# Copying the strided operands of dilated attention scores into contiguous tiles

## The chip, the cores and the metric

One NeuronCore of one Trainium2 chip runs the whole program in one launch. The metric is the device time in microseconds (us); the kernel was run several times and the median counts. One more execution was taken with the profiler on, and all rows shown here are from that one.

## The reference

A decoder trunk of two layers on a sequence of 2048 tokens with 1024 features, in float32. The second layer has, beside four retention heads, eight heads of dilated attention of 64 features each. The part that matters here:

```
DIL_PATTERNS = ((128, 1), (512, 4), (2048, 16))      # (window, dilation)

for window, dil in DIL_PATTERNS:
    # query t attends keys t, t-dil, ..., t-window (causal)
    # tokens are gathered by residue class mod dil, then cut into blocks of 128 queries
    s = q_block @ [previous block | own block of keys].T / 8
    p = exp(s - max), den = sum(p), o = p @ v / den, lse = max + log(den)
o = sum over patterns of softmax(lse) * o
```

With dilation 1 there are 16 blocks of consecutive tokens. With dilation 4 a block is every fourth token of a stretch of 512, so there are four stretches with four residues each. With dilation 16 a block is every sixteenth token of the whole sequence, and there is no previous block.

## The kernel before, in words

**Number format.** Products that need float32 accuracy are made from f16 numbers split into a high and a low part. A head's operands are in one SBUF tile, `st`, of shape [128 partitions, 3, 2048 tokens]. `st[:, 0]` holds the queries, their high part in partitions 0 to 63 and their low part in 64 to 127; `st[:, 1]` the keys' high part in both halves, `st[:, 2]` the keys' low part in both. Two matmuls per score block (lines 892 and 893), one with `st[:, 1]` and one with `st[:, 2]`, add up to the score. For dilation 4 and 16 both take their queries and keys out of `st` with a step of 4 or 16 tokens.

**Groups.** `groups(h)` makes 12 groups of four score blocks for head h: 0 to 3 for dilation 1 (pattern 0), 4 to 7 for dilation 4 (pattern 1, one stretch of 512 tokens each, four residues), 8 to 11 for dilation 16 (pattern 2, four residues each). A score block is 128 queries by 256 keys (128 where there is no previous block). The order within a head is 4 to 11, then 0 to 3.

**One group.** `scores` runs eight matmuls on TensorE into a PSUM tile `big` (two buffers); VectorE adds the mask and takes the row maximum (L895), and makes the bias (L898); ScalarE takes the exponential and the row sum (L899) and converts to f16, `dl_ph` (L901); VectorE subtracts to get the low part, `dl_pl` (L902); two DMA transposes issued by SyncE bring both into `dl_pt` (L903, L904). `values`, two groups later (`LAG`), multiplies `dl_pt` with the values on TensorE (L914, L915), and ScalarE (L918) and VectorE (L921) write the sum of the two halves of the result into the head's record `dl_rec`. Records of patterns 1 and 2 go through device memory to be put in token order (L928, L929, issued by GpSimd). `mixed` joins the three patterns (L935 to L955; the products of L952 run on GpSimd). `dl_ph`, `dl_pl`, `dl_pt` and the score tile `dl_s` have two buffers each; `dl_o1` has one.

**What runs between the groups.** `periods` and `merge` put other units of work between the groups of a head, by a written cost: the projection of the next head (`Heads.tiles`: products of `co.rows`, L164 to L166, then rope on VectorE, L762 to L765, an addition on GpSimd, L766, evacuation on ScalarE, L406 and L407, and DMA transposes into the next head's `st`, L421) and projections of the gate and of the retention inputs (`Extra.rows`: the same products, evacuation by ScalarE, L230 or L233, and a store issued by GpSimd, L234). These projections go through the PSUM tile `dn` (two buffers).

**Order.** The program is written in this order, and the framework (`TileContext(..., schedule_with_timeline_sim=True)`) sets every semaphore and decides at build time, with its own estimates of durations, in which order each engine gets its instructions. At run time each engine works through its own list in order, and an instruction that waits holds up those behind it. A tile name with k buffers can be given out again when the last reader of the tile k allocations before is done.

Of the kernel before, what the change touches and what calls it, by code (L numbers as in the profile page):

```python
# [7 lines left out]
F32 = mybir.dt.float32  # L8
F16 = mybir.dt.float16
BF16 = mybir.dt.bfloat16  # L10
I32 = mybir.dt.int32
AF = mybir.ActivationFunctionType
# [5 lines left out]
S = 2048  # L18
# [831 lines left out]
def dilated(co, work, keep, heads, cst, v_d, rec_d, mix_d):  # L850

    nc = co.nc
    mask = work.tile([128, 256], F32, name="dl_mask", bufs=1)
    nc.sync.dma_start(mask, cst["c_dmask"])
    recs, live = {}, {}

    def groups(h):
        v1 = heads.v[h]
        nc.gpsimd.dma_start(v_d[h].rearrange("(t p) n -> p t n", p=128), v1)
        v2 = work.tile([128, 4, 4, 128], F16, name="dl_v2", bufs=1)  # L860
        nc.gpsimd.dma_start(v2, v_d[h].rearrange("(b i r) n -> i b r n", b=4, r=4))
        v3 = work.tile([128, 16, 128], F16, name="dl_v3", bufs=1)
        nc.gpsimd.dma_start(v3, v_d[h].rearrange("(i r) n -> i r n", r=16))
        out = []
        for t0 in range(0, NT, 4):
            ts = [1, 2, 3, 0] if t0 == 0 else range(t0, t0 + 4)
            out.append((0, [(t, slice(128 * t, 128 * t + 128), slice(128 * max(t - 1, 0), 128 * t + 128),
                             [v1[:, k, :] for k in ((t - 1, t) if t else (0,))]) for t in ts]))
        for b in range(4):
            out.append((1, [(4 * b + r, slice(512 * b + r, 512 * b + 512, 4),  # L870
                             slice(512 * max(b - 1, 0) + r, 512 * b + 512, 4),
                             [v2[:, k, r, :] for k in ((b - 1, b) if b else (0,))]) for r in range(4)]))
        for r0 in range(0, 16, 4):
            out.append((2, [(r, slice(r, S, 16), slice(r, S, 16), [v3[:, r, :]]) for r in range(r0, r0 + 4)]))
        recs[h] = [keep.tile([128, NT, 66], F32, name=f"dl_rec{i}", bufs=2 if i == 1 else 1) for i in range(3)]
        return out

    def scores(h, g, pat, units):
        rec, st, f = recs[h][pat], heads.st[h], heads.f[h]
        p = co.ps([128, 1024], "big")  # L880
        raw = work.tile([128, 1024], F32, name="dl_s")
        ph = work.tile([128, 1024], F16, name="dl_ph")
        pl = work.tile([128, 1024], F16, name="dl_pl")
        pt = work.tile([128, 2, 8, 128], F16, name="dl_pt")
        m = co.small.tile([128, 4], F32, name="dl_m")
        at, spans = 0, []
        for n, qs, ks, vs in units:
            width = 128 * len(vs)
            sp = slice(at, at + width)
            spans.append(sp)  # L890
            at += width
            nc.tensor.matmul(p[:, sp], st[:, 0, qs], st[:, 1, ks], start=True, stop=False)  # L892
            nc.tensor.matmul(p[:, sp], st[:, 0, qs], st[:, 2, ks], start=False, stop=True)  # L893
        for i, ((n, _, _, vs), sp) in enumerate(zip(units, spans)):
            nc.vector.tensor_tensor_reduce(  # L895
                out=raw[:, sp], in0=p[:, sp], in1=mask[:, 256 - 128 * len(vs):], scale=f[:, 0:1],
# [10 lines left out]
    def values(h, g, pat, units):  # L907
# [3 lines left out]
        for i, ((n, _, _, vs), sp) in enumerate(zip(units, spans)):  # L911
            for k, x in enumerate(vs):
# [1 line left out]
                nc.tensor.matmul(pv[:, i, :], pt[:, 0, kt, :], x, start=k == 0, stop=False)  # L914
                nc.tensor.matmul(pv[:, i, 0:64], pt[:, 1, kt, :], x[:, 0:64], start=False,  # L915
                                 stop=k == len(vs) - 1)
        o1 = work.tile([128, 4, 64], F32, name="dl_o1", bufs=1)
        nc.scalar.activation(o1, pv[:, :, 0:64], AF.Copy)  # L918
        ns = [un[0] for un in units]
        if ns == sorted(ns):  # L920
            nc.vector.tensor_add(rec[:, ns[0]:ns[0] + 4, 0:64], pv[:, :, 64:128], o1)  # L921
        else:
            nc.vector.tensor_add(rec[:, 1:4, 0:64], pv[:, 0:3, 64:128], o1[:, 0:3, :])
            nc.vector.tensor_add(rec[:, 0:1, 0:64], pv[:, 3:4, 64:128], o1[:, 3:4, :])
        if pat and g % 4 == 3:
            rd = rec_d[h, pat - 1]
            lay = ("(b i r) n -> i b r n", "(i b r) n -> i b r n")[pat - 1]
# [292 lines left out]
```

## Time and profile before

| what | us |
|---|---|
| median of 3 runs | 2388.01 (2387.26 to 2394.36) |
| the profiled execution, its own time | 2393.75 |
| span of the profiled execution, first to last instruction | 2391.7 |
| TensorE (PE) busy in the span | 2186.1 |
| VectorE (DVE) busy | 1549.6 |
| ScalarE (ACT) busy | 1121.3 |
| GpSimd (POOL) busy | 531.3 |
| dilated scores, first to last matmul | 1272.0 to 2062.0 |

PE is TensorE's matmuls, PEld its weight loads, DVE is VectorE, ACT ScalarE, POOL GpSimd, SP SyncE; a q behind an engine's name means its sequencer, which issues DMAs and waits. L892 is line 892 of the kernel before. Matmuls overlap: the duration of one is longer than the distance to the next.

### The profile page before, as it was taken

What the parts mean: (1) busy time and instruction counts of PE and PEld (TensorE: products, weight loads), DVE (VectorE), ACT (ScalarE), POOL (GpSimd) and SP (SyncE); (2) the same over time, 40 slices, a digit from 0 to 9 for tenths busy, and PEclk for the clock granted to TensorE, in tenths of its full rate; (3) what the DMA queues carried; (4) which work ended last, traced back from release to release, by engine and by line L of the source; (5) the groups of instructions that cost most, each with busy time, mean ns of one, the idle gap of its engine ahead of it and who ended that gap; (6) DMA issues with size and microseconds to landing.
All of it is one profiled execution on the core that took longest, in us unless ns stands there. A gap on an engine that the chain in (4) does not pass through costs nothing. (4 is left out here: it accounts for less than half of the span.)

```text
span 2391.7 us, 51539 instructions
## 1 busy us (share of the span) xinstructions
PE 2186.1 (91%) x19956; PEld 1694.2 (71%) x19956; DVE 1549.6 (65%) x4870; ACT 1121.3 (47%) x2580; POOL 531.3 (22%) x638
## 2 busy tenths in 40 slices
PE   4888799998999999999999998999998799889998
PEld 3666687676687878754448978888887688765454
DVE  5447666666676768566557675667574667687674
ACT  5445445454555546345444544555453445533332
POOL 0012211212212012111112122231322122145441
PEclk9799899999999999999999999999998899989999
DMA  9958888988898867888877687786786858966653
GB/s 203 177 109 152 150 152 151 176 151 144 157 162 167 152 141 181 217 194 211 216 168 143 138 143 149 136 165 145 143 145 120 139 114 159 168 214 181 178 171 106
DMA packets 840501, 381.87 MB, mean 160 GB/s; under 512 B 743088, under 2 KB 799296, under 8 KB 840000
## 3 DMA queue, kind: packets, MB, share of 16 engines
q1 hardware_dynamic: 742832, 259.29, 57.6%
q0 software_dynamic: 23584, 82.33, 12.6%
q10 hardware_dynamic: 73840, 36.97, 6.5%
q8 instruction: 156, 2.56, 0.4%
q14 instruction: 89, 0.73, 0.1%
HBM read 135.40 MB, written 73.73 MB: 87 GB/s over the span
## 5 line engine op out<-in xcount | busy, mean ns | idle before, releaser
L164 PE MATMUL dn<-w,uh 128*128 128x192 f16 (+1 forms) x3840 | 1010.4, 263 | 19.1 <-DVE x_out L231 6.6
L166 PE MATMUL dn<-w,ul 128*128 128x192 f16 (+1 forms) x3840 | 1009.0, 263 | 4.7 <-DMA ul<-u_lo 4.7
L165 PE MATMUL dn<-w,uh 128*128 128x192 f16 (+1 forms) x3840 | 1009.5, 263 | 0.0
L164 PEld LDWEIGHTS <-uh 128*128 128x128 f16 x3968 | 394.3, 100 | 54.4 <-DMA uh<-u_hi 16.2
L166 PEld LDWEIGHTS <-ul 128*128 128x128 f16 x3968 | 392.1, 100 | 42.4 <-DMA ul<-u_lo 15.3
L165 PEld LDWEIGHTS <-uh 128*128 128x128 f16 x3968 | 393.3, 100 | 35.6 <-issue 7.5
L516 ACT ACTIVATE fx_s<-fx_s,fx_nm 128x1152 f32<-128x1152 f32 (+15 forms) x128 | 152.7, 1194 | 182.0 <-DVE fx_nm L514 182.0
L899 ACT ACTIVATE dl_s<-dl_s,dl_m 128x256 f32<-128x256 f32 (+1 forms) x384 | 172.6, 451 | 118.7 <-DVE dl_m L898 103.4
L521 DVE TENSOR_TENSOR fx_pl<-fx_s,fx_ph 128x2176 f16<-128x2176 f32 x64 | 155.0, 2423 | 82.0 <-DMA fx_tl<-fx_pl 47.9
L895 DVE CUSTOM_DVE_ANT_0 dl_s<-big,dl_mask,hd_f 128x256 f32<-128x256 f32 (+1 forms) x384 | 141.7, 420 | 52.9 <-PE big L893 51.8
L508 DVE CUSTOM_DVE_ANT_0 fx_s<-big,cb,hd_f 128x1024 f32<-128x1024 f32 (+7 forms) x128 | 133.6, 1044 | 34.5 <-PE big L506 20.2
L79 POOL TENSOR_TENSOR rs_r<-rs_v,mhalf 128x1 f32<-128x1 f32 (+2 forms) x96 | 67.4, 706 | 396.4 <-DVE rs_v L76 377.3
L902 DVE TENSOR_TENSOR dl_pl<-dl_s,dl_ph 128x512 f16<-128x512 f32 (+2 forms) x96 | 100.5, 1049 | 78.7 <-ACT dl_ph L901 58.5
L520 ACT ACTIVATE fx_ph<-fx_s 128x2176 f16<-128x2176 f32 x64 | 128.8, 2012 | 32.9 <-DMA fx_th<-fx_ph 25.5
L503 PE MATMUL big<-head 128*128 128x512 f16 (+3 forms) x320 | 113.2, 354 | 28.0 <-DVE fx_m L508 27.9
L85 DVE SCALAR_TENSOR_TENSOR w<-w_raw,w_gs,w 128x256 f16<-128x256 f32 (+2 forms) x296 | 123.9, 472 | 12.4 <-ACT w L84 12.3
L892 PE MATMUL big<-head 128*128 128x256 f16 (+1 forms) x384 | 129.5, 355 | 0.6 <-DVE dl_rec L895 0.6
L893 PE MATMUL big<-head 128*128 128x256 f16 (+1 forms) x384 | 129.7, 357 | 0.0
L84 ACT ACTIVATE w<-w_raw,w_gs 128x256 f16<-128x256 f32 (+2 forms) x296 | 113.5, 466 | 30.5 <-DVE w_gs L145 23.1
L536 PE MATMUL aux<-head,fx_tl 128*128 128x64 f16 x1088 | 105.7, 197 | 22.8 <-DMA fx_tl<-fx_pl 22.7
L535 PE MATMUL aux<-head,fx_th 128*128 128x128 f16 x1088 | 110.4, 224 | 16.9 <-DMA fx_th<-fx_ph 16.9
L547 POOL TENSOR_TENSOR fx_o<-fx_o 128x64 f32<-128x64 f32 x128 | 46.3, 381 | 333.8 <-DVE fx_o L541 193.1
(235 smaller groups left out, 4332.1 us busy)
## 6 DMA issues: line engine op xcount, KB each, us to landing
gate_d<-x_out POOLq DMA_DIRECT2D x64, 256.0 KB, 4.0
o_gate<-gate_d SPq DMA_DIRECT2D x32, 512.0 KB, 4.4
rec_d<-dl_rec POOLq DMA_DIRECT2D x16, 528.0 KB, 5.4
dl_rec<-rec_d POOLq DMA_DIRECT2D x16, 528.0 KB, 6.1
x_h<-in_x_dram SPq DMA_DIRECT2D x16, 512.0 KB, 4.6
cb<-cum_d SPq DMA_DIRECT2D x16, 512.0 KB, 10.3
o_mix<-mix_d SPq DMA_DIRECT2D x32, 256.0 KB, 3.0
o_h<-in_x_dram SPq DMA_DIRECT2D x16, 512.0 KB, 4.6
```

Source lines behind the costliest of these rows:

```text
L85: self.nc.vector.scalar_tensor_tensor(lo, x, scale, hi, op0=OP.mult, op1=OP.subtract)
L164: nc.tensor.matmul(out, uh[:, k, xs], wh[:, k, c0:c1], start=k == 0, stop=False)
L165: nc.tensor.matmul(out, uh[:, k, xs], wl[:, k, c0:c1], start=False, stop=False)
L166: self.last = nc.tensor.matmul(out, ul[:, k, xs], wh[:, k, c0:c1], start=False, stop=k == KT - 1)
L508: nc.vector.tensor_tensor_reduce(out=x[:, at + c * 1024:at + c * 1024 + wide], in0=p[:, :wide], in1=cb[c][:, :wide], scale=f[:, 0:1], scal ...
L516: nc.scalar.activation(x[:, sp], x[:, sp], AF.Exp, bias=nm[:, part:part + 1], accum_out=nm[:, 2 + part:3 + part])
L520: nc.scalar.activation(ph, x[:, 0:W], AF.Copy)
L521: nc.vector.tensor_sub(pl, x[:, 0:W], ph)
L892: nc.tensor.matmul(p[:, sp], st[:, 0, qs], st[:, 1, ks], start=True, stop=False)
L893: nc.tensor.matmul(p[:, sp], st[:, 0, qs], st[:, 2, ks], start=False, stop=True)
L895: nc.vector.tensor_tensor_reduce(out=raw[:, sp], in0=p[:, sp], in1=mask[:, 256 - 128 * len(vs):], scale=f[:, 0:1], scalar=-3.0e38, op0=OP. ...
L899: nc.scalar.activation(raw[:, sp], raw[:, sp], AF.Exp, bias=m[:, i:i + 1], accum_out=rec[:, n, 65:66])
```

## The change

For patterns 1 and 2 a new function, `stage`, copies a group's queries (`dl_gq`, one buffer) and both key parts (`dl_gk`, two buffers) out of `st` into tiles in which the 128 tokens of a score block are contiguous. GpSimd makes the copies. The score matmuls read these tiles. Since the previous key block of a dilation-4 group lies in the tile of the group before, a block of 256 keys is computed as two of 128, with two matmuls each. `dl_ph` and `dl_pl` go from two buffers to one. The tile `dl_o1` goes: ScalarE writes the first half of the values' result straight into the record and VectorE adds the second half in place; where the group's blocks are out of order (the first group of pattern 0) both do it in two pieces.

```diff
-    recs, live = {}, {}
+    recs, live, staged = {}, {}, {}
...
         for b in range(4):
-            out.append((1, [(4 * b + r, slice(512 * b + r, 512 * b + 512, 4),
-                             slice(512 * max(b - 1, 0) + r, 512 * b + 512, 4),
+            out.append((1, [(4 * b + r, None, None,
                              [v2[:, k, r, :] for k in ((b - 1, b) if b else (0,))]) for r in range(4)]))
         for r0 in range(0, 16, 4):
-            out.append((2, [(r, slice(r, S, 16), slice(r, S, 16), [v3[:, r, :]]) for r in range(r0, r0 + 4)]))
+            out.append((2, [(r, None, None, [v3[:, r, :]]) for r in range(r0, r0 + 4)]))
...
+    def stage(h, g):
+
+        st = heads.st[h]
+        src = (st[:, :, 512 * (g - 4):512 * (g - 3)].rearrange("p s (i r) -> p s r i", r=4) if g < 8
+               else st.rearrange("p s (i r) -> p s r i", r=16)[:, :, 4 * (g - 8):4 * (g - 7), :])
+        ks = work.tile([128, 2, 4, 128], F16, name="dl_gk")
+        nc.gpsimd.tensor_copy(ks, src[:, 1:3])
+        qs = work.tile([128, 4, 128], F16, name="dl_gq", bufs=1)
+        nc.gpsimd.tensor_copy(qs, src[:, 0])
+        staged[h, g] = qs, ks
+
     def scores(h, g, pat, units):
         rec, st, f = recs[h][pat], heads.st[h], heads.f[h]
+        if pat:
+            stage(h, g)
         p = co.ps([128, 1024], "big")
         raw = work.tile([128, 1024], F32, name="dl_s")
-        ph = work.tile([128, 1024], F16, name="dl_ph")
-        pl = work.tile([128, 1024], F16, name="dl_pl")
+        ph = work.tile([128, 1024], F16, name="dl_ph", bufs=1)
+        pl = work.tile([128, 1024], F16, name="dl_pl", bufs=1)
...
-            nc.tensor.matmul(p[:, sp], st[:, 0, qs], st[:, 1, ks], start=True, stop=False)
-            nc.tensor.matmul(p[:, sp], st[:, 0, qs], st[:, 2, ks], start=False, stop=True)
+            if pat == 0:
+                nc.tensor.matmul(p[:, sp], st[:, 0, qs], st[:, 1, ks], start=True, stop=False)
+                nc.tensor.matmul(p[:, sp], st[:, 0, qs], st[:, 2, ks], start=False, stop=True)
+                continue
+            q = staged[h, g][0][:, n % 4, :]
+            for i in range(len(vs)):
+                ks = staged[h, g - len(vs) + 1 + i][1]
+                kp = slice(sp.start + 128 * i, sp.start + 128 * (i + 1))
+                nc.tensor.matmul(p[:, kp], q, ks[:, 0, n % 4, :], start=True, stop=False)
+                nc.tensor.matmul(p[:, kp], q, ks[:, 1, n % 4, :], start=False, stop=True)
...
-        o1 = work.tile([128, 4, 64], F32, name="dl_o1", bufs=1)
-        nc.scalar.activation(o1, pv[:, :, 0:64], AF.Copy)
         ns = [un[0] for un in units]
-        if ns == sorted(ns):
-            nc.vector.tensor_add(rec[:, ns[0]:ns[0] + 4, 0:64], pv[:, :, 64:128], o1)
-        else:
-            nc.vector.tensor_add(rec[:, 1:4, 0:64], pv[:, 0:3, 64:128], o1[:, 0:3, :])
-            nc.vector.tensor_add(rec[:, 0:1, 0:64], pv[:, 3:4, 64:128], o1[:, 3:4, :])
+        for a, b in ((0, 4),) if ns == sorted(ns) else ((0, 3), (3, 4)):
+            to = rec[:, ns[a]:ns[b - 1] + 1, 0:64]
+            nc.scalar.activation(to, pv[:, a:b, 0:64], AF.Copy)
+            nc.vector.tensor_add(to, pv[:, a:b, 64:128], to)
```

## Rows read from the trace of the kernel before

**Rows 1.** The page, busy engines, and TensorE's granted clock in 40 slices.
```profile
PE 2186.1 (91%) x19956; PEld 1694.2 (71%) x19956; DVE 1549.6 (65%) x4870; ACT 1121.3 (47%) x2580; POOL 531.3 (22%) x638
...
PEclk9799899999999999999999999999998899989999
```

**Rows 2.** Windows: stretch, length, busy us per engine, clock, DMA share.
```profile
1272.00:2070.00 798.00, 747.83 (x7619) 660.64 (x7617) 530.95 (x2216) 409.44 (x1266) 188.50 (x202) 0.97 0.75 142
2070.00:2392.00 322.00, 293.94 (x1688) 169.10 (x1685) 217.58 (x630) 101.90 (x196) 129.11 (x108) 0.96 0.60 169
```

**Rows 3.** Waits of TensorE, 1272 to 2070: total us, times, longest.
```profile
PE aux L914 <- DMA dl_pt<-dl_ph: 23.4, 3, 11.2
PE aux L915 <- DMA dl_pt<-dl_pl: 22.8, 13, 5.9
```

**Rows 4.** Timeline of TensorE: start, duration; a pattern-1 group with 256 keys.
```profile
1607.04 0.39 PE L892 MATMUL big<-head 128*128 128x256 f16 x1
...
1608.86 0.29 PE L164 MATMUL dn<-w,uh 128*128 128x256 f16 x1
```

**Rows 5.** Timeline of TensorE: a pattern-1 group with 128 keys.
```profile
1586.28 0.28 PE L892 MATMUL big<-head 128*128 128x128 f16 x1
...
1587.20 0.24 PE L914 MATMUL aux<-head,dl_pt 128*128 128x128 f16 x1
```

**Rows 6.** Timeline of TensorE: a pattern-2 group.
```profile
1625.47 0.40 PE L892 MATMUL big<-head 128*128 128x128 f16 x1
...
1627.37 0.27 PE L164 MATMUL dn<-w,uh 128*128 128x192 f16 x1
```

**Rows 7.** Timeline of TensorE: a value pair, then a pattern-0 group.
```profile
1352.89 0.22 PE L914 MATMUL aux<-dl_v,dl_pt 128*128 128x128 f16 x1
...
1352.97 0.22 PE L914 MATMUL aux<-dl_v,dl_pt 128*128 128x128 f16 x1
...
1353.22 0.27 PE L892 MATMUL big<-head 128*128 128x256 f16 x1
...
1353.88 0.22 PE L892 MATMUL big<-head 128*128 128x128 f16 x1
...
1353.99 0.27 PE L164 MATMUL dn<-w,uh 128*128 128x256 f16 x1
```

**Rows 8.** Groups by line and shape, GpSimd: busy us, mean ns, idle before.
```profile
L482 POOL TENSOR_SCALAR cb<-cb,hd_f 128x1024 f32<-128x1024 f32 x16 | 46.7, 2919 | 90.7 <-DMA cb<-cum_d 84.3 <-PE dn L166 6.4
L952 POOL TENSOR_TENSOR dl_rec<-dl_rec,dl_es 128x1024 f32<-128x1024 f32 x24 | 46.5, 1956 | 42.0 <-DVE dl_es L949 18.6 <-ACT dl_o L918 9.4 <-DVE dl_m L898 7.8
...
L234 POOL DMA_DIRECT2D qkv_d<-x_out x32 | 23.3, 728 | 114.2 <-ACT x_out L233 85.9 <-ACT dl_o L918 28.4
...
L929 POOL DMA_DIRECT2D dl_rec<-rec_d x16 | 18.9, 1179 | 67.4 <-DMA rec_d<-dl_rec 42.3 <-issue 8.2 <-DVE dl_rec L924 5.8
```

**Rows 9.** Waits of GpSimd, 1272 to 2070: total us, times, longest.
```profile
POOL qkv_d L234 <- ACT x_out L233: 85.9, 20, 7.3
...
POOL dl_rec L929 <- DMA rec_d<-dl_rec: 42.3, 10, 12.7
```

**Rows 10.** Waits of ScalarE, 1272 to 2070.
```profile
ACT dl_ph L901 <- DMA dl_pt<-dl_ph: 38.5, 7, 15.7
```

**Rows 11.** The tile dl_ph: durations as min, median, max ns; landing of its transposes.
```profile
L901 ACT ACTIVATE dl_ph<-dl_s x96: 612/996/1061, 1286.0 to 2072.7; 128x1024 f16<-128x1024 f32 x48, 128x512 f16<-128x512 f32 x40, 128x896 f16<-128x896 f32 x8
...
DMA to landing us min/median/max: 2.4/3.5/18.5
```

**Rows 12.** Waits of SyncE's DMA queue, 1272 to 2070.
```profile
SPq L903 <- PE aux L915: 145.7, 40, 12.6
```

**Rows 13.** Timelines of VectorE and GpSimd near 1592 us; line 902 in all.
```profile
1592.48 1.24 DVE L902 TENSOR_TENSOR dl_pl<-dl_s,dl_ph 128x512 f16<-128x512 f32 x1 [1.27 <-ACT dl_ph L901]
...
1591.28 4.21 POOL L952 TENSOR_TENSOR dl_rec<-dl_rec,dl_es 128x1024 f32<-128x1024 f32 x2 [2.17 <-DVE dl_es L949]
...
L902 DVE TENSOR_TENSOR dl_pl<-dl_s,dl_ph x96: 675/1210/2780, 1291.3 to 2073.8; 128x1024 f16<-128x1024 f32 x48, 128x512 f16<-128x512 f32 x40, 128x896 f16<-128x896 f32 x8
```

## The prediction

> **What bounds the kernel now.** I read the page first: TensorE is busy 91% of the span and its granted clock is close to full in nearly all of the 40 slices [rows 1]. Then I cut the span into stretches. All the scores that the change touches run between 1272 and 2070 us, one third of the span, which I call the stage. In it TensorE is busy 748 of 798 us at a clock of 0.97, VectorE 531, ScalarE 409 and GpSimd 188 [rows 2]. So TensorE sets the pace of the stage and the others have room; the 322 us behind it hold none of the changed work. The waits of TensorE tell where its missing 50 us are: 23.4 and 22.8 us before the value products, on the transposes that bring the probabilities into dl_pt [rows 3]. The reader should keep that in mind, because the change touches the buffers in front of these transposes.
>
> **What the scores cost.** Matmuls overlap, so I take the distance from start to start. Eight matmuls of pattern 1 with 256 strided columns (every 4th element) take from 1607.04 to 1608.86, 1.82 us [rows 4]. In its first block, with 128 columns, eight take 0.92 us [rows 5]. Eight of pattern 2 with 128 columns (every 16th element) take 1.90 us [rows 6]. Pattern 0 reads contiguous columns in the same stage: six matmuls of 256 columns take 0.66 us, 0.11 each, and two of 128 take 0.11, 0.055 each [rows 7]. Stride 4 costs about twice, stride 16 about four times the contiguous time per column.
>
> The Trainium skill (SBUF — State Buffer, the note on SBUF cachelines under the DMA port swizzle) says that two accesses per 16-byte line keep the full rate, which a step of four f16 elements satisfies. By that rule only pattern 2 would gain, 4 x (1.90 - 0.44) x 8 = 47 us. The trace does not agree: at that step it shows 0.23 us where 256 contiguous columns take 0.11, and the measurement decides.
>
> **Removed from TensorE.** A head has three pattern-1 groups of 1.82, one of 0.92 and four pattern-2 groups of 1.90: 13.98 us. After the change every matmul has 128 contiguous columns. The three groups become 16 matmuls each (the two key blocks now lie in different tiles), the other five have eight: 48 + 40 = 88 matmuls x 0.055 = 4.84 us. One fear is the doubled weight loads of the 16-matmul groups; a value pair of 128 and 64 columns with two loads goes by in 0.08 us [rows 7], so loads at this rate do not hold back a matmul of 0.055. Saved: 9.14 us a head, 73 us over eight heads, on the engine that paces the stage.
>
> **Added on GpSimd.** Each of 64 groups gets a copy of 1,024 elements a partition (keys, high and low) and one of 512 (queries). No such copy is in the trace. The nearest rows are two-input products of 1,024 elements at 1.96 us and a one-input scaling of 1,024 at 2.92 us [rows 8]. Half of the two-input price, one operand instead of two, is my lower bound: 0.96 ns an element; the scaling is the upper bound: 2.85. I take 1.91, the row with the plainest loop: 2.9 us a group (bounds 1.5 and 4.4), 188 us in all (94 to 281). GpSimd would be busy 376 of some 725 us. That is hidden as long as each copy is done when TensorE comes to its scores.
>
> The query tile has one buffer and the key tiles have two, of which the previous one is still read; so the copies for group g wait for the scores of g-1. Scores come every 798 / 96 = 8.3 us, 7.5 us if all is saved. Less the scores' own time some 6.6 us are left for 2.9. Ahead of a copy in GpSimd's order can stand a read-back of records (L929), which waited ten times for its write to land, 42.3 us in all, longest 12.7 [rows 9]: 4.2 + 1.2 of its own + 2.9 is 1.7 too much, so 10 x 1.7 = 17 us that TensorE waits (bounds: nothing, and the 73 of the third rival). I charge the stores of x_out (4.3 us mean wait) at nothing: what they wait for comes earlier in TensorE's order too; without that cover it is the third rival. Behind a waiting copy stand the rope additions (L766), which feed only the next head, and the stores, which free x_out, hence ScalarE's evacuation, hence the PSUM of the projections.
>
> **Single buffers for dl_ph and dl_pl.** ScalarE's conversion of a group (L901) must now wait until the transpose of the group before has landed. Behind it on ScalarE stand the next exponentials and the evacuations that free PSUM for TensorE's projections; behind VectorE's L902, which waits in the same way, stand the score reductions and the rope products, which free PSUM as well. With two buffers ScalarE already waited 38.5 us for it in seven cases, once 15.7 [rows 10]. The conversion has a median of 1.0 us, the landing one of 3.5, 18.5 at worst [rows 11]. The transposes also wait to be issued: 40 of them waited 145.7 us, 3.6 each, for value products that free dl_pt [rows 12]. In these 40 the buffer is free after 1.0 + 3.6 + 3.5 = 8.1 us against a step of 7.5: 0.6 x 40 = 24 us. For the late landings I charge the 38.5 us once more. ScalarE is then late by 62 us in sum. It is idle for over 40% of the stage and TensorE has two PSUM buffers of projections in hand, so I let a third reach TensorE, 20 us; bounds are nothing and, if every wait for dl_pt reaches it, 146 us.
>
> **The rest.** Writing the high half of the values into the record and adding in place keeps one ScalarE and one VectorE instruction a group; in the one group a head that VectorE already split, ScalarE gets one instruction more, eight in all, hidden under its 389 idle us of the stage. The shared tile that goes can only have made ScalarE wait for VectorE, and neither sets the pace: nothing either way.
>
> VectorE loses time to GpSimd. A subtraction of 512 elements took 1.24 us while GpSimd ran two products, against 0.68 at best, and another subtraction took 2.78 [rows 13]. Copies would run in 188 of 725 us, 26%. I estimate that one of the 96 subtractions that meets a copy waits about 1 us of it: 96 x 0.26 x 1 = 25 us, and as much again for VectorE's other work with two SBUF inputs: 581 of 725. The bounds are nothing and all 188, which would make it 719. At 581 it still does not pace the stage: nothing, unless the rival below holds.
>
> The Trainium skill (SBUF — State Buffer, Who interferes with whom) says that a VectorE instruction with two SBUF inputs and a GpSimd instruction that reads SBUF exclude each other for the whole instruction. By that rule a copy can hold VectorE back for all of its length, the upper bound just named. The trace agrees in the 1.24 us.
>
> **Sum.** -73 + 17 + 20 = -36 us. The profiled execution took 2393.75 us (span 2391.7), 5.7 over the median of 2388.0; from the median I get 2352 us.
>
> **The rivals.** *Full gain* (2315 us): the 73 us arrive whole because the planner that orders each engine's instructions knows the new buffers and spreads the groups. For it: TensorE waited only some 50 us in the stage. Against: GpSimd and ScalarE both get waits that are long in the trace.
>
> *VectorE becomes the bound* (2376): it is held back by the whole 188 us of copies and sets the pace at 719 us busy; with the 50 us that TensorE idles in the stage today that is 769 against 798, a gain of 29, of which the 17 us of waits for copies take their share: 12. For it: the 1.24 and 2.78 us. Against: VectorE has most of its work from PSUM, with one SBUF input.
>
> *GpSimd's order cancels the gain* (2388): if a copy stands behind a store that waits, 4.3 + 0.7 + 2.9 = 7.9 us against 6.6; if all 64 copies are late by 1.1 us, 73 us are gone. For it: the stores waited 20 times for ScalarE [rows 9]. Against: that needs every group.
>
> *Slower, by the single dl_ph buffer*: TensorE's value products free dl_pt, the transpose lands, only then ScalarE converts the next group and goes on to the evacuations that TensorE needs. This loop through TensorE has a price of up to 146 us. After 73 - 17 = 56 us of it, 38%, reach TensorE, the gain is gone; with three quarters the time is 2388 - 56 + 109 = 2441 us. For it: ScalarE's longest wait here is 15.7 us with two buffers [rows 10]. Against: ScalarE has room between.
>
> That the strided reads stay slow as copied tiles is excluded by pattern 0, in the same stage with the same shapes.
>
> **How the numbers follow.** Forecast 0.40 (own range 2335 to 2375), full gain 0.18, VectorE 0.10, GpSimd 0.12, single buffer 0.20. A change of 0.3%, 7 us, is what a measurement here tells from none. Faster: 0.40 + 0.18 + 0.10 = 0.68; same 0.12; slower 0.20. The range reaches from just under the full gain, 2312, into the slower case, 2405, leaving out some 0.04 below and 0.14 above.
>
> **What would show it.** Scores of patterns 1 and 2 at 0.055 us start to start, 88 a head. GpSimd copies near 1.9 and 1.0 us. TensorE waiting for the copies for about 17 us. ScalarE's wait for dl_ph's landing near 100 us instead of 38.5, VectorE's L902 longer. The dilated stage near 760 us instead of 798, and the 322 us behind it unchanged. The prediction is wrong if the copies take 4 us or more, if TensorE's busy share in the stage falls below 85%, or if ScalarE's waits show up one to one as TensorE's.

## The result: 2497.8 us, slower by 4.9%

The changed kernel took 2497.82 us (median of 4 runs, 2497.74 to 2518.92) against 2391.19 (2387.26 to 2396.35) of the kernel before on the same chip: ratio 1.0494, 95% interval 1.0445 to 1.0543 (the ratio is estimated from the single runs; the quotient of the two medians is 1.045). The forecast was 2352, with a range of 2312 to 2405.

The page of the profiled execution after, busy engines and TensorE's granted clock, beside [rows 1]:

```profile
PE 2169.8 (87%) x20148; PEld 1691.8 (68%) x20148; DVE 1597.7 (64%) x4870; ACT 1116.1 (45%) x2588; POOL 692.4 (28%) x766
...
PEclk8899899999999999999999898999989898859999
```

The span is 2496.1 us, before it was 2391.7. TensorE is busy 16.3 us less than before (2186.1 to 2169.8) and idle 120.7 us more (205.6 to 326.3). These two numbers are the whole change of the span, +104.4. The windows after, columns as in [rows 2]:

```profile
1272.00:2172.00 900.00, 750.56 (x8112) 679.80 (x8112) 582.66 (x2233) 412.84 (x1288) 355.46 (x337) 0.93 0.66 130
2172.00:2496.00 324.00, 278.11 (x1380) 150.53 (x1380) 212.47 (x610) 93.57 (x180) 122.86 (x100) 0.85 0.53 156
```

The stage grew from 798 to about 900 us. The stretch behind it kept its length (324, before 322) but not its work: it holds 1380 matmuls instead of 1688, at a clock of 0.85 instead of 0.96, so that the forecast "unchanged" came true here by accident. TensorE is busy 83% of the stage, and its clock is 0.93 instead of 0.97.

The score matmuls themselves are what the prediction said. Timeline of TensorE, a pattern-1 group of 16 matmuls, to be laid beside [rows 4]:

```profile
1313.39 0.22 PE L912 MATMUL big<-dl_gk,dl_gq 128*128 128x128 f16 x1
...
1314.28 0.25 PE L164 MATMUL dn<-w,uh 128*128 128x192 f16 x1
```

0.89 us instead of 1.82. The copies are cheaper than assumed, 164.5 us in all instead of 188. Groups by line and shape, GpSimd, 1250 to 2180:

```profile
L883 POOL COPY dl_gk<-head 128x1024 f16<-128x1024 f16 x64 | 104.4, 1639 | 110.6 <-DMA head<-qk_x 44.1 <-PE big L913 36.5 <-issue 29.9
...
L885 POOL COPY dl_gq<-head 128x512 f16<-128x512 f16 x64 | 60.1, 939 | 60.3 <-PE big L913 41.0 <-issue 12.0 <-DMA head<-qk_x 5.5
```

And TensorE hardly ever waits for a copy. Its waits from 1250 to 2200, beside [rows 3] (over this longer stretch the two rows of before are 29.1 and 23.9 us, and the head's drains, L411, are not among its waits):

```profile
PE aux L934 <- DMA dl_pt<-dl_ph: 62.6, 27, 7.4
PE aux L935 <- DMA dl_pt<-dl_pl: 53.0, 23, 8.5
PE dn L164 <- DVE head L411: 21.6, 10, 7.1
...
PE big L912 <- POOL dl_gk L883: 4.0, 1, 4.0
```

The copy is waited for once, 4.0 us. What grew are the waits for the probabilities in dl_pt (53.0 to 115.6 us) and for VectorE's drains of the projections (to 21.6). Waits of ScalarE for the single dl_ph, beside [rows 10], and of VectorE for the single dl_pl, 1272 to 2180:

```profile
ACT dl_ph L921 <- DMA dl_pt<-dl_ph: 61.6, 21, 10.0
...
DVE dl_pl L922 <- DMA dl_pt<-dl_pl: 88.9, 25, 13.7
```

**Where a head starts.** GpSimd's timeline at the first head:

```profile
1270.69 0.64 POOL L885 COPY dl_gq<-head 128x512 f16<-128x512 f16 x1 [5.52 <-DMA head<-qk_x]
...
1302.58 0.79 POOL L861 DMA_DIRECT2D dl_v<-v_d  x1 [3.61 <-DMA head<-qk_x]
...
1303.91 2.18 POOL L883 COPY dl_gk<-head 128x1024 f16<-128x1024 f16 x2
```

The copy of the queries runs at 1270.69, as soon as the first 512 tokens are in `st`. The copy of the keys of the same tokens runs 33 us later. Each 512 tokens come into `st` by three transposes (L421): queries, high keys, low keys. Those of the head's last tokens landed at 1302.5, 1302.9 and 1304.9, and the key copy starts between the second and the third. It takes `st[:, 1:3]` of 512 tokens in one access; from its first element to its last this spans all 2048 tokens of the high part and only the first 512 of the low part, so it was ordered behind transposes whose data it does not read. The other heads show the same: in all eight the first key copy starts 0.1 to 1.0 us after the head's last high-part transpose has landed, 0.3 to 7.3 us before the last low-part one has, and 25 to 46 us after the first query copy. The second head shows what can come of it. Windows after, around its first scores:

```profile
1390.00:1400.00 10.00, 8.89 (x84) 7.88 (x82) 2.86 (x8) 2.32 (x10) 2.28 (x3) 0.86 1.19 172
1400.00:1406.00 6.00, 0.00 (x0) 0.00 (x0) 0.00 (x0) 0.00 (x0) 0.41 (x1) 0.75 1.03 137
1406.00:1413.00 7.00, 5.51 (x39) 5.05 (x40) 1.85 (x6) 1.64 (x2) 4.56 (x5) 0.50 0.66 149
```

For 6 us TensorE, VectorE and ScalarE stand still and GpSimd nearly so; only DMA works. In SyncE's queue the transposes into dl_pt and the last one into the next head's `st` stand one behind the other, and two of them take 6.55 and 5.00 us to issue:

```profile
1392.03 6.55 SPq L923 DMA_TRANSPOSE dl_pt<-dl_ph  x1
1398.62 1.79 SPq L421 DMA_TRANSPOSE head<-qk_x  x1
1400.45 5.00 SPq L924 DMA_TRANSPOSE dl_pt<-dl_pl  x1
```

TensorE's next instruction is a value product, L934, which waits 7.4 us for dl_pt, the longest wait of its row above. GpSimd's next is the key copy. The last high-part transpose of the head, issued at 1390.34, took 15.1 us to land, so until 1405.4 (first fence, that one transpose alone), and the copy starts 0.2 us later:

```profile
L421 SPq DMA_TRANSPOSE head<-qk_x x1: 1528/1528/1528, 1390.3 to 1390.3; - x1
...
DMA to landing us min/median/max: 15.1/15.1/15.1
```

```profile
1405.59 2.13 POOL L883 COPY dl_gk<-head 128x1024 f16<-128x1024 f16 x2 [12.75 <-issue]
```

Then TensorE runs at a granted clock of 0.50, its lower level (1.2 GHz), and the first scores go at half pace (timeline of TensorE):

```profile
1411.30 0.31 PE L912 MATMUL big<-dl_gk,dl_gq 128*128 128x128 f16 x1
1411.41 0.31 PE L913 MATMUL big<-dl_gk,dl_gq 128*128 128x128 f16 x1
```

0.11 us from start to start, not 0.056. Before, scores of this head ran at 1387.5, with TensorE busy 10.00 of the 10 us from 1385 at a clock of 1.00.

### The profile page after: what moved, and what is told of

It is laid out like the page before. It is cut to its first block, busy times and chain, and to the rows that moved or that the text cites. A ratio compares the mean times of both kernels' runs of the same rounds, so it can differ in the third digit from the quotient of the medians.

```text
span 2496.1 us, 52047 instructions
## 1 busy us (share of the span) xinstructions
PE 2169.8 (87%) x20148; PEld 1691.8 (68%) x20148; DVE 1597.7 (64%) x4870; ACT 1116.1 (45%) x2588; POOL 692.4 (28%) x766
## 5 line engine op out<-in xcount | busy, mean ns | idle before, releaser
L164 PE MATMUL dn<-w,uh 128*128 128x192 f16 (+1 forms) x3840 | 1021.0, 266 | 45.1 <-DVE head L411 25.9
L166 PE MATMUL dn<-w,ul 128*128 128x192 f16 (+1 forms) x3840 | 1021.0, 266 | 4.7 <-DMA ul<-u_lo 4.7
L165 PE MATMUL dn<-w,uh 128*128 128x192 f16 (+1 forms) x3840 | 1021.1, 266 | 0.0
L164 PEld LDWEIGHTS <-uh 128*128 128x128 f16 x3968 | 398.3, 101 | 74.6 <-DVE head L411 23.9
L166 PEld LDWEIGHTS <-ul 128*128 128x128 f16 x3968 | 397.2, 101 | 45.3 <-DMA ul<-u_lo 16.8
L85 DVE SCALAR_TENSOR_TENSOR w<-w_raw,w_gs,w 128x256 f16<-128x256 f32 (+2 forms) x296 | 132.7, 504 | 9.7 <-ACT w L84 9.5
L883 POOL COPY dl_gk<-head 128x1024 f16<-128x1024 f16 x64 | 104.4, 1639 | 110.6 <-DMA head<-qk_x 44.1
L133 DVE TENSOR_REDUCE w_am<-w_raw 128x8 f32<-128x2048 f32 (+2 forms) x41 | 83.1, 2028 | 56.6 <-DMA w_raw<-in_w_in_even_dram 25.3
```

The costliest lines, as they stand in the source:

```text
L85: self.nc.vector.scalar_tensor_tensor(lo, x, scale, hi, op0=OP.mult, op1=OP.subtract)
L164: nc.tensor.matmul(out, uh[:, k, xs], wh[:, k, c0:c1], start=k == 0, stop=False)
L165: nc.tensor.matmul(out, uh[:, k, xs], wl[:, k, c0:c1], start=False, stop=False)
L166: self.last = nc.tensor.matmul(out, ul[:, k, xs], wh[:, k, c0:c1], start=False, stop=k == KT - 1)
```

## The experiments

All times are medians, each ratio is to runs of the kernel before on the same chip, with its 95% interval. The ratios are estimated from the single runs, and the medians come from different chips, so a difference of two medians and that of two ratios can be up to 14 us apart. "Idle" is span less busy time of TensorE, "work" its busy time times the mean clock, a rough measure in us at full clock. These four columns are of one profiled execution each, while the runs of one kernel spread over up to 38 us.

```
                      median   ratio  interval          busy   idle  clock  work
before                2388.01                          2186.1  205.6  0.963  2105
changed               2497.82  1.0494 1.0445..1.0543   2169.8  326.3  0.936  2031
e1_single             2402.34  1.0053 1.0024..1.0082   2189.8  199.5  0.964  2111
e2_contig             2343.77  0.9819 0.9765..0.9873   2122.5  216.7  0.959  2035
e3_contig_single      2382.35  0.9983 0.9946..1.0021   2136.9  232.8  0.957  2045
e4_record             2370.30  0.9929 0.9896..0.9961   2190.7  178.1  0.960  2103
f1_two_buffers        2513.79  1.0545 1.0493..1.0596   2164.8  346.7  0.936  2026
f2_vector             2425.43  1.0164 1.0128..1.0200   2144.2  273.7  0.950  2037
f3_other_source       2441.36  1.0229 1.0195..1.0262   2158.0  282.3  0.945  2039
f4_unread             2455.33  1.0276 1.0232..1.0320   2158.5  283.3  0.946  2042
h1_split_copy         2433.13  1.0165 1.0130..1.0201   2158.9  277.0  0.944  2038
h2_split_vector       2392.18  1.0019 0.9991..1.0048   2136.1  252.0  0.956  2042
h3_split_vector_two   2378.63  0.9970 0.9933..1.0007   2142.3  245.3  0.952  2039
h4_unread_other       2504.50  1.0470 1.0438..1.0502   2175.7  319.0  0.937  2039
k1_memset             2374.07  0.9951 0.9917..0.9985   2138.8  242.2  0.951  2034
l1_memset_twice       2374.28  0.9931 0.9900..0.9963   2145.4  231.7  0.951  2040
k2_pattern2_vector    2390.48  1.0030 1.0005..1.0054   2162.9  233.2  0.952  2059
l2_pattern2_free_half 2389.56  1.0002 0.9974..1.0031   2167.6  219.9  0.949  2057
k3_pattern2_scalar    2398.46  1.0050 1.0018..1.0082   2167.2  223.2  0.952  2063
k4_split_scalar_two   2398.09  1.0044 1.0024..1.0065   2148.8  242.9  0.950  2041
```

The framework orders the instructions anew for each kernel, so a difference between two of them holds the edit and the new order. Only two pairs have, on TensorE, VectorE, ScalarE and GpSimd, the same order instruction by instruction: before and e2, and e1 and e3.

**The parts alone, on the kernel before.** e1: the single low and high tiles.

```diff
-        ph = work.tile([128, 1024], F16, name="dl_ph")
-        pl = work.tile([128, 1024], F16, name="dl_pl")
+        ph = work.tile([128, 1024], F16, name="dl_ph", bufs=1)
+        pl = work.tile([128, 1024], F16, name="dl_pl", bufs=1)
```

> The kernel before with one buffer each for dl_ph and dl_pl and nothing else changed. Theory S (the single buffers cost the time: the conversions wait for the transposes, the transposes come late, TensorE waits for dl_pt and its clock drops): slower than before by 100 to 175 us, VectorE's wait of L902 for the landing of dl_pl's transposes near 89 us instead of 20, TensorE's waits for dl_pt near 110 us instead of 46. Theory G (the copies on GpSimd cost it, by its queue and by holding VectorE back): within 20 us of before.

It costs 13 us by its ratio, within the 20 of theory G and far from theory S. ScalarE's wait goes from 38.5 us [rows 10] to (same stretch)

```profile
ACT dl_ph L901 <- DMA dl_pt<-dl_ph: 83.7, 29, 9.1
```

while TensorE idles no more than before. The profiled execution, at 2391.1, is the fastest of its runs, so it does not show where the 13 us are.

e2: the score matmuls of patterns 1 and 2 read contiguous columns of `st` in the same number and widths, other data; nothing is copied. e3: e2 with e1's single tiles.

```diff
-            out.append((2, [(r, slice(r, S, 16), slice(r, S, 16), [v3[:, r, :]]) for r in range(r0, r0 + 4)]))
+            out.append((2, [(r, slice(128 * r, 128 * r + 128), slice(128 * r, 128 * r + 128), [v3[:, r, :]]) for r in range(r0, r0 + 4)]))
```

> The kernel before with the slices of patterns 1 and 2 replaced by contiguous ones of the same widths (other tokens, so the scores of these patterns are of other blocks), no copies, two buffers. What the contiguous reads are worth by themselves: by the prediction's sum about 73 us faster, 2318 us, if TensorE paces the stage. If TensorE's time is only replaced by waits for dl_pt, theory W: under 30 us faster.

> As the run with contiguous slices (scores of patterns 1 and 2 of other blocks, no copies), but with single buffers of dl_ph and dl_pl. Theory S: the same loss as the single buffers alone bring, so about 100 to 175 us slower than the contiguous run with two buffers, near the changed kernel's 2498 us. Theory G: about 2340 to 2350 us; the remaining 150 us are then the copies'.

e2 is the ceiling of the idea: 43 us faster by its ratio, in the same order, between the two values expected. TensorE's work falls by 70, as costed, but its busy time by 64 (the clock falls to 0.959), and it idles 11 us more, though its waits for dl_pt are little longer (57.8 us, before 53.0). These are of one execution each, and the one before was 5.7 us above its median. With single tiles 39 of the 43 are gone (e3).

e4: the record write alone, without dl_o1.

> The kernel before with the high half of the values written into the record and added in place (no dl_o1), nothing else. Both theories: within 7 us of before. A third theory R: the write into the record makes ScalarE wait for readers of the record and costs 20 us or more.

17 us faster by its ratio, which no theory had. ScalarE's wait for dl_ph's landing falls to 17.6 us, TensorE's waits for dl_pt from 53.0 to 35.3. But e4 has an order of its own, so whether the edit or the order did it is open. Of the versions that leave nothing of the computation out it is the fastest.

**What in the changed kernel costs.** f1: two buffers of dl_ph again, the low part written in place into the score tile. f2: the copies on VectorE. f3: the copies read a tile that is ready long before (`uh`), so nothing waits for the head; the scores are of other data. f4: the copies are made, the matmuls read contiguous columns of `st` instead.

```diff
@@ f1
+        pl = raw.bitcast(F16)[:, 0:1024]
@@ f2
+        nc.vector.tensor_copy(ks, src[:, 1:3])
@@ f3
+        x = heads.u[0][0].rearrange("p k n -> p (k n)")
@@ f4
+            q = st[:, 0, 512 * b0 + 128 * (n % 4):512 * b0 + 128 * (n % 4) + 128]
```

> The changed kernel with two buffers again for both halves: dl_ph has two, and the low half is written into the score tile dl_s, which has two, in place (the changed kernel with a second buffer for dl_ph and dl_pl does not fit). Theory C (the copies on GpSimd cost about 130 us through their waits and their place in the order, whatever the buffers): about 40 us less than the changed kernel, near 2455. Theory I (copies and single buffers are bad only together): back under 2400, near 2345 if the contiguous reads then arrive.

> The changed kernel with the copies on VectorE instead of GpSimd. Theory C1 (GpSimd's in-order queue and its slow copies): about 2370 to 2400, since VectorE copies f16 faster and has room. Theory C2 (any staged copy that waits for the head's last transposes and for the scores before costs the same): still above 2460. If VectorE becomes the bound: between, with VectorE busy over 85% of the stage.

> The changed kernel with GpSimd's copies taken from the layer's input tile uh, which has long landed, with the same steps and sizes (the scores of patterns 1 and 2 are of other data). Theory C2a (a copy at the start of a head waits on GpSimd for the head's last transposes, and the queue behind it and the scores start late): the loss goes, below 2420. Theory C1 (the copies' occupancy and order): still 2470 or more.

> The changed kernel, all copies made on GpSimd as in it, but the score matmuls read contiguous slices of st of the same width (scores of patterns 1 and 2 of other blocks), so nobody waits for the copies. Theory C3 (TensorE's scores come late because they wait for the copies): near the contiguous single-buffer kernel, 2370 to 2390. Theory C1 (the copies hold up GpSimd's other work, the rope additions and stores): still above 2450.

f1 is no faster than the changed kernel (16 us slower by the medians, with overlapping intervals): two buffers give nothing back here. Its low part lies in the score tile, so it is not the exact reverse of the edit. By the medians f2 gains 72, f3 56, f4 42 (by the ratios 79, 63, 52). Each takes away one part, and none comes near 2368, the sum of e2, the 39 us of e3 and e4 (2389 - 43 + 39 - 17). So none of these parts alone is the loss.

**The key copy in two.** h1: the high and the low keys copied one by one, still by GpSimd. h2: so too, on VectorE. h3: h2 with f1's tiles.

```diff
-        nc.gpsimd.tensor_copy(ks, src[:, 1:3])
+        for i in range(2):
+            nc.gpsimd.tensor_copy(ks[:, i], src[:, 1 + i])
```

> The changed kernel with the key copy of each group made as two copies, high part and low part, on GpSimd (three copies a group instead of two). Theory D (the one copy over both parts is ordered behind the head's last transposes, since its range runs over the later tokens of the high part; the query copy of the first group, which reads one part, ran 33 us earlier in the first head): the first score of a head comes before the head's last landing again and some 57 us, as with the other source, come back: 2430 to 2450. Theory C2 (any copy waits that long): unchanged, 2498 or a little more.

> As the split copy, with all copies on VectorE. Theory D with C1 (GpSimd's queue and its slow copies cost the rest): 2425 less most of 57, about 2370, below the kernel before. If the wait is not worth it on VectorE: 2420.

> As the split copy on VectorE, with two buffers for dl_ph and the low half written in place into dl_s. If the single buffers cost 39 us as they did between the two contiguous kernels: 2330 to 2340, the best so far. If the buffers cost nothing here, as in the changed kernel: as the split copy on VectorE.

h1 alone gives back 65 us (79 by the ratios), as theory D said. GpSimd's timeline at the first head shows the two key copies right behind the query's; in all eight heads the first key copy now starts 36 to 55 us before the head's last high-part transpose lands:

```profile
1274.02 0.63 POOL L886 COPY dl_gq<-head 128x512 f16<-128x512 f16 x1 [7.01 <-DMA head<-qk_x]
1274.60 0.63 POOL L884 COPY dl_gk<-head 128x512 f16<-128x512 f16 x1
1276.02 0.65 POOL L884 COPY dl_gk<-head 128x512 f16<-128x512 f16 x1
```

The dilated part starts 23 us earlier, ends 56 us earlier and is 33 us shorter. First and last conversion to dl_ph, in the changed kernel and in h1 (before: 1286.0 to 2072.7 [rows 11]):

```profile
L921 ACT ACTIVATE dl_ph<-dl_s x96: 612/996/1059, 1312.3 to 2173.7; 128x1024 f16<-128x1024 f32 x48, 128x512 f16<-128x512 f32 x40, 128x896 f16<-128x896 f32 x8
```

```profile
L922 ACT ACTIVATE dl_ph<-dl_s x96: 613/995/1057, 1289.6 to 2118.2; 128x1024 f16<-128x1024 f32 x48, 128x512 f16<-128x512 f32 x40, 128x896 f16<-128x896 f32 x8
```

Whether the 23 us at the first head are part of the gain is not shown: from 1250 to 1320 TensorE is busy 65.1 us in the changed kernel and 65.2 in h1. Its waits for dl_pt fall from 115.6 to 79.2 us, those for VectorE's drains from 21.6 to 8.7; but the order differs too.

VectorE instead of GpSimd (h2) gives 41 more, and the kernel is where it was before the change. TensorE's waits for the drains do not carry these 41 us (1250 to 2200, h1, then h2):

```profile
PE dn L164 <- DVE head L411: 8.7, 6, 2.8
```

```profile
PE dn L164 <- DVE head L411: 7.1, 7, 3.1
```

Nor do the prices add up: with the joint copy VectorE in place of GpSimd is worth 72 us (f2), and on VectorE the split is worth 33 (f2 to h2). h3 takes 14 us less than h2, with overlapping intervals, where 2330 to 2340 was expected if two buffers were worth 39.

**Copies against memsets.** h4 is f3 and f4 together: GpSimd copies from `uh`, unread, so no copy waits for the head and no matmul for a copy. k1 has memsets of the same tiles in place of these copies, l1 each memset twice.

```diff
-        nc.gpsimd.tensor_copy(ks, src[:, -2:] if g >= 8 else src[:, 1:3])
+        nc.gpsimd.memset(ks, 0.0)
```

> The changed kernel with GpSimd's copies from the input tile uh and not read by TensorE, which reads contiguous slices of st (scores of patterns 1 and 2 of other blocks): GpSimd's time for the copies alone, no wait on the head and nobody waiting. Theory C1 (occupancy and order of GpSimd): still 2430 or more. Theory D with C3 (only the waits cost): 2360 to 2385, like the contiguous single-buffer kernel with the record's write.

> The 64 + 64 GpSimd copies of the dilated scores become memsets of the same two tiles, which no matmul reads (the matmuls read contiguous columns of st), so GpSimd writes the tiles and reads nothing; the scores are not the reference's. Beside h4_unread_other (2504.5 us), which differs only in that its GpSimd instructions are copies. Theory 'a GpSimd copy holds VectorE, or is held by it, while both read and write SBUF': with nothing read and shorter instructions the time comes back to about 2365 (contiguous reads, single low and high tiles, record write: 2389 - 45 + 39 - 18), at most 2400, and VectorE's drains of the head (L409 by the line of before) are back near 35 us in all. Rival 'the place in GpSimd's queue': the memsets wait for the same buffers to come free (none here, since nothing reads them) and stand at the same places, so if order is what costs, at least 2450.

> As k1_memset (2374.1 us), with each memset issued twice: GpSimd's added work goes from 90 to about 180 us, more than the 158 us of the copies of h4_unread_other (2504.5 us), at the same places in its queue; the scores are not the reference's. Theory 'a GpSimd copy costs by what it reads and writes beside VectorE, not by the time it takes in its own queue': 2370 to 2400, and no waits of TensorE for the head's drains (L411) over some 10 us. Rival 'the length of GpSimd's added work delays the rotation's products and the write-backs behind it': 2450 or more, with 40 us or more of those waits.

h4 is as slow as the changed kernel, 2504.5, though nothing waits for its copies, and though f3 and f4, of which it is made, each gained 42 us or more; k1 takes 2374.1, and l1, whose GpSimd work is longer than that of the copies, 2374.3. So neither GpSimd's time nor a wait for the copies costs h4 its 130 us. What the memsets lack is the read; the order differs too. VectorE is busy 1642.0 us in h4 and 1559.3 in k1, with the same 4870 instructions. Waits of TensorE (1250 to 2180) in h4, then k1:

```profile
PE dn L164 <- DVE head L411: 61.5, 19, 10.0
```

```profile
PE dn L164 <- DVE head L411: 2.3, 3, 1.3
```

And VectorE's rope product L409 and its copy L414, as min, median, max ns, in h4, k1, and l1:

```profile
L409 DVE SCALAR_TENSOR_TENSOR qk_x<-dl_r,qk_x x124: 221/284/4678, 1275.6 to 2087.4; 128x128 f16<-128x128 f32 x124
...
L414 DVE COPY qk_x<-qk_x x31: 206/219/7036, 1293.4 to 2087.6; 128x256 f16<-128x256 f16 x31
```

```profile
L409 DVE SCALAR_TENSOR_TENSOR qk_x<-dl_r,qk_x x124: 270/283/479, 1273.2 to 1969.0; 128x128 f16<-128x128 f32 x124
...
L414 DVE COPY qk_x<-qk_x x31: 214/220/3624, 1279.9 to 1969.2; 128x256 f16<-128x256 f16 x31
```

```profile
L409 DVE SCALAR_TENSOR_TENSOR qk_x<-dl_r,qk_x x124: 272/284/2321, 1273.3 to 1963.7; 128x128 f16<-128x128 f32 x124
...
L414 DVE COPY qk_x<-qk_x x31: 213/222/3629, 1279.9 to 1963.9; 128x256 f16<-128x256 f16 x31
```

L409 reads two SBUF tiles. In h4 one of them took 4.7 us instead of 0.28, while GpSimd ran a copy of 2.0 us and a product of 1.9 one behind the other; beside the memsets it took 0.48 at most in k1, and 2.3 at most in l1. Summed over the program the 128 of them took 36.4 us before and in k1, 49.7 in the changed kernel, 53.5 in h1, 36.2 in h2 and 70.3 in h4. The f16 copy L414 is held by both, 7.0 and 3.6 us (before 0.5 at most here). The Trainium skill (SBUF — State Buffer, Who interferes with whom) says that a VectorE instruction with two SBUF inputs excludes a GpSimd instruction that reads SBUF but not one that only writes, and that VectorE's copies, which can run in a two-port mode, exclude any; the rows agree. The 2.3 us in l1 do not speak against it: there two L409 end at 1398.09, right behind L145, a TENSOR_SCALAR of VectorE that ran until 1398.08 beside the memsets (timeline of VectorE in l1):

```profile
1392.44 5.64 DVE L145 TENSOR_SCALAR w_gs<-g_odd,w_s 128x8 f32<-128x8 f32 x1
1395.77 2.32 DVE L409 SCALAR_TENSOR_TENSOR qk_x<-dl_r,qk_x 128x128 f16<-128x128 f32 x2
```

That VectorE is held is shown. That this is all of the 130 us is not: the order of h4 differs from that of k1 too.

**A version that keeps the gain?** k2: only pattern 2 staged, split copies on VectorE, f1's tiles, the record write. k3: k2 with the copies on ScalarE. k4: h3 with the copies on ScalarE. l2: k2 with the staged keys in the half of the score tile that pattern 2 leaves free, so that dl_ph and dl_pl have two buffers each and nothing is in place.

```diff
+        pl = work.tile([128, 1024], F16, name="dl_pl")
+        if pat == 2:
+            stage(h, g, raw.bitcast(F16)[:, 1024:2048].rearrange("p (s r i) -> p s r i", s=2, r=4))
```

> Only the stride-16 units (pattern 2) are staged, with the high and the low key copied one by one, on VectorE; pattern 1 reads st with stride 4 as before; two buffers of the high part, the low part written in place, the record write as in the change. Theory 'what is left of the gain is eaten by the first copy of a head standing behind its transposes and by the time the copies take of another engine': pattern 2 comes last in a head, so its copies are late for nothing; it holds 4 x (1.90 - 0.44) x 8 = 47 of the 73 us, of which six tenths arrive as in e2_contig (29), and the record write gives 18: 2389 - 29 - 18 = about 2342, 2335 to 2365 with VectorE's half of the 105 us of copies (some 50 us more busy there) not quite hidden. Rival 'any copy costs what it saves': 2370 or more, as the record write alone gave 2370.

> As k2_pattern2_vector, with the three copies of a group on ScalarE. ScalarE is the least busy of the three after GpSimd in this stage but does the exp between the scores and the weights, so a copy of some 1 to 2 us in its queue delays an exp. Theory 'the copies cost by what they delay in the engine they stand in': 2345 to 2375, not better than k2. Rival 'VectorE is the engine that is short': better than k2 by 10 us or more.

> As h3_split_vector_two (2378.6 us: both patterns staged, high and low copied apart, on VectorE, two buffers), with the copies on ScalarE. Theory 'the first key copy of a head no longer waits for the last transposes, and the copies cost by the engine that they stand in': within 20 us of h3 either way, 2365 to 2400; below 2365 would say that VectorE is what is short in h3, above 2400 that ScalarE is, since its queue holds the exps.

> As k2_pattern2_vector (2390.5 us), with the staged keys in the half of the fp32 score tile that the 512-column groups of pattern 2 leave free, so that dl_ph and dl_pl both keep their two buffers and the low part is not written in place. Theory 'k2 lost its gain to the low part in place, whose tile is held until its transpose has read it (54.6 us of VectorE idle behind that DMA)': 2335 to 2360 (2370 of the record write alone less six tenths of 47 us, some of it lost to 60 us more on VectorE). Rival 'any copy costs what it saves, through VectorE's own queue': 2365 to 2395.

None does, and none is faster than before. k2 and l2 (2390) miss their 2335 to 2365 and 2335 to 2360 and land where the rival put them; the true two buffers of l2 gain nothing over k2. k3 (2398) is not better than k2, and k4 (2398) is 20 us above h3. In l2 TensorE's work falls by 48, as costed for pattern 2 (47), and by 46 against e4; yet it is 17 us slower than e4 by the ratios, because TensorE idles 42 us more (178.1 to 219.9) and runs at 0.949 instead of 0.960, which takes back half of the work in busy time (only 23 us less).

## Why the prediction was wrong

**The removed work (-73) was right, what it is worth was not.** Work at full clock fell by 74 in the changed kernel. Alone, in an unchanged order and without copies, that is 43 us of time (e2). The prediction put the whole saving on the engine that paces the stage; in e2 TensorE had 70 us less work, but was busy only 64 us less and idle 11 us more.

**The copies (+17): the step that failed.** It was "That is hidden as long as each copy is done when TensorE comes to its scores", with a price for ten copies behind read-backs. TensorE waited 4.0 us for a copy, and yet the changed kernel is 124 us slower than k1, which has memsets in their place. Two things were left out of this step.

First, what a copy itself must wait for. The prediction had "the copies for group g wait for the scores of g-1" and no wait for the head's transposes; in every head the first joint key copy comes only when the last high-part transpose has landed, 33 us later than the first query copy in the first head, and splitting it gives 65 us back (h1).

Second, what a GpSimd copy does to VectorE. The size was right: the prediction let VectorE lose some 50 us, to 581 in the stage, and with the same 4870 instructions it is busy 1597.7 us instead of 1549.6, and 582.7 in the stage. What failed is the price of nothing, because VectorE "does not pace the stage". It does not have to: TensorE's projections need its drains one by one, and waited 21.6 us for them here and 61.5 in h4. Between h1 and h2, 41 us apart, these waits are nearly equal (8.7 and 7.1), so what those 41 us are stays open.

**The single tiles (+20): mis-sized.** 13 us with strided reads (e1), 39 with contiguous ones (e3 against e2), inside the bounds. In the changed kernel they add nothing that f1 could give back.

**The record write (0):** -17 in e4, cause open.

**The clock was charged with nothing.** Here, too, one execution each: k1 gives TensorE the same number and shapes of matmuls as the changed kernel and has it busy 2138.8 us at 0.951; in the changed kernel it is 2169.8 at 0.936. 31 us of slowing come with the idle time, as at 1406; behind the stage the clock is 0.50 from 2172 to 2200, where TensorE is busy 8.4 of 28 us.

**The sum.** k1, with all of the change but the copies' reads and the waits for them, stands at 2374, near the 2368 of the parts. The copies add 124 to it. On the way over h1 and h2 these are 65 (joint access), 41 (GpSimd in place of VectorE) and 18 (VectorE's copies); on the way over f2 and h2 they are 72, 33 and 18. These are differences of kernels with different orders, not prices of three causes.

**The rivals.** None was it. "Slower, by the single dl_ph buffer" fell with f1; "GpSimd's order" named the right engine, but its copies were to be late behind stores, and the copies were not what TensorE waited for. *VectorE becomes the bound* had the engine that is held, but VectorE lost 48 us and not 188, and is busy 64% of the span. Of the signs that the prediction named, TensorE's busy share of under 85% came (83%); ScalarE's wait for dl_ph's landing became 61.6 us and not 100.

**What stays open** is how much of these prices acts at run time and how much through the order. Here are, of some 5,570 to 5,890 projection matmuls between the first scores and the last values, in the order in which TensorE was given its instructions, those that stand where exactly one group is scored and not yet multiplied with its values:

```
before, e2   268      h1   874      k1  233      f4  241
e4           201      f3   568      l1  233      h4  137
changed     1981      f1  1819      h2  234      f2  243
```

In the changed kernel and f1 the values stand close behind their scores, with less work between to cover the transposes, and these two have the longest waits for dl_pt. This suggests, and does not show, that part of their loss is laid down when the kernel is built, where joint copies of the head are made on GpSimd and read. h4 and f4 have no such order and are slow all the same, with the longest waits for VectorE's drains (61.5 and 32.4 us). No kernel with the order of before and the copies was run, so the two shares aren't separated.

## What to carry to other kernels

Before moving work to an idle engine, ask what the moved instruction must wait for as the framework sees its access, from first element to last, and not only whether it is done in time: one access over several parts of a tile waits for the writes to all that lies between. A copy that GpSimd makes can be paid by VectorE's instructions with two SBUF inputs, even where VectorE has room on average. And run the ceiling first, here the reads made contiguous with nothing copied: 43 us, of which single tiles take 39, left too little to pay for any of the copies tried.

## What the runs showed of the hardware

GpSimd's copy of 1,024 f16 elements a partition takes twice as long with a source step of 16 elements as with 4. Its timeline, a pattern-1 and a pattern-2 copy:

```profile
1417.45 1.09 POOL L883 COPY dl_gk<-head 128x1024 f16<-128x1024 f16 x1
...
1459.20 2.04 POOL L883 COPY dl_gk<-head 128x1024 f16<-128x1024 f16 x1
```

A memset of the same tile took 0.96. And in every kernel whose scores read contiguous columns, of both patterns or of pattern 2 alone, TensorE's mean clock was lower: 0.93 (changed) to 0.957 (e2) in the median of its runs, against 0.960 of the kernel before. So part of each saving comes back as slower matmuls.
